# State-space input laid out through DRAM, phase tables as one tile, read-out matrices earlier on POOL

## The chip, the cores and the metric

The kernel runs on one core of a Trainium2 chip. The core has a matrix engine (TensorE, PE in the profile), a vector engine (VectorE, DVE), a scalar engine (ScalarE, ACT), GpSimd (POOL) and SyncE (SP), which issues the transfers here. Each engine works through its own queue of instructions in order; between engines semaphores hold an instruction back until its inputs are there and the memory it writes is free. The metric is the device time of one execution in microseconds (us); lower is better.

## What is computed

The reference is one layer of a diffusion backbone for 128 context and 512 latent tokens (640 columns in all) of width 1024. Of the combined projection `z = h @ w_in` come the inputs of three mixers: attention, a bidirectional linear recurrent unit (`lru`), and a bidirectional state-space mixer (S5). Only the last one is changed:

```python
lam_bar = jnp.exp(lam * step)
b_bar = ((lam_bar - 1.0) / lam)[..., None] * b_mat[None]
bu = jnp.einsum('blgp,dgnp->dblgn', u32.astype(jnp.complex64), b_bar)
for d, reverse in enumerate((False, True)):
    a = jnp.broadcast_to(lam_bar[d], bu[d].shape)
    h, h_last = linear_scan(a, bu[d], h0[:, d], reverse)
    y = y + jnp.einsum('blgn,gpn->blgp', h, c_mat[d]).real
```

After it come the merge gates, the output projection and a convolutional feed-forward network, which take the rest of the time.

## The kernel before

Activations lie with the width on the 128 partitions and the 640 tokens along the free axis. Each large product is made of three products of split operands: `hh`/`hl` are the high and low part of an activation, `sh`/`sl` those of a weight block. For each block of weights SP loads `wr` (512 KB), ACT writes `sh`, DVE writes `sl = wr - sh`, and PE multiplies; so PE asks ACT, DVE and SP for something every few microseconds in the whole kernel.

The state-space mixer works on four tokens at a time (160 columns of four). Its parts, in order of the program:
- `u`, the mixer's input: two products of 128 rows; ACT copies each out of PSUM into `usb`, and 16 copies on DVE (L660) spread it into `ut`, where token 0 to 3 of a group of four stand on four blocks of 32 partitions. `usb` has the tag `xh` with one buffer, so the `xh` of the first `lru` tile lies in the same memory and is written after the last copy.
- `s5_prepare`: for each direction `d`, POOL clears `vt` (L334), DVE fills it with 8 copies, 12 products and 12 sums, PE forms `gp` from it and transposes it into `vm`; at the end DVE and ACT assemble `km`.
- `s5_tables` (DVE): the phase tables `tab0` and `tab1`, real and imaginary powers for 160 columns, by doubling: from n columns the next n, in blocks of 16 at most, each block with six operations through two scratch tiles `tq`; five small operations square the power.
- `s5_cl` (POOL): the read-out matrices `cl`, in eight rounds of two products into scratch tiles and four sums into `cl`, 48 operations. Its scratch tiles have the tags of the tables' scratch.
- `s5_half`, twice, each for two directions: PE multiplies `vm` by `ut`, ACT moves the result to `v`, DVE rotates it by the tables, scans it twice and rotates it back to `sr` and `si` (this is called a chain here: from `v<-v,lh0r` to `si`), and PE sums `ut,km`, `sr,cl` and `si,cl`.

The order of POOL's queue is that of the program (`manual_schedule`); the other queues are ordered by a scheduler that knows of costs. The program itself interleaves the preparation (`p`) with the two `lru` tiles by the string `ORDER`, and between any two steps `fill()` emits independent work (gate products, modulation, the attention's values):

```python
    for g in ORDER:
        next(gens[g], None)
        fill()
```

The pool `pst`, with `vt` and the other tiles of the preparation, is closed before `ptab`, the pool of the tables, is opened; both take memory from the same side.

Of the kernel before, what the change touches and what calls it, by code (L numbers as in the profile page):

```python
# [11 lines left out]
F32 = mybir.dt.float32  # L12
# [8 lines left out]
P = 128  # L21
# [17 lines left out]
KPOW = 1  # L39
NB = 2  # L40
# [29 lines left out]
def tile_hybrid_flow_step(ctx, tc, a, o):  # L70
# [241 lines left out]
    def s5_prepare(pst):  # L312
# [11 lines left out]
        t4 = [pst.tile(sh, F32, name=f"q{i}") for i in range(4)]  # L324
# [175 lines left out]
    vct = pv.tile([P, 512], F32, name="vct")  # L500
    tsp = [pd.tile([P, NT], F32, name=f"tsp{i}") for i in range(24)]
# [237 lines left out]
    tab = [ptab.tile([P, 16, 160], F32, name=f"tab{q}") for q in range(2)]  # L739

    def s5_tables(e):

        er, ei = tab
        V.memset(er[:, :, 0:1], 1.0)
        V.memset(ei[:, :, 0:1], 0.0)
        p_r, p_i = unit
        n = 1
        while n < 160:
            for z in range(0, min(n, 160 - n), 16):
                m = min(16, n - z)  # L750
                tmp = [ptab.tile([P, 16, 16], F32, tag=f"tq{q}", name="tq") for q in range(2)]
                br = p_r.unsqueeze(2).to_broadcast([P, 16, m])
                bi = p_i.unsqueeze(2).to_broadcast([P, 16, m])
                t0, t1 = (t[:, :, 0:m] for t in tmp)
                tt(t0, er[:, :, z:z + m], br, MUL, e)
                tt(t1, ei[:, :, z:z + m], bi, MUL, e)
                tt(er[:, :, n + z:n + z + m], t0, t1, SUB, e)
                tt(t0, er[:, :, z:z + m], bi, MUL, e)
                tt(t1, ei[:, :, z:z + m], br, MUL, e)
                tt(ei[:, :, n + z:n + z + m], t0, t1, ADD, e)  # L760
            n *= 2
            if n < 160:
                q = [pl.tile([P, 16], F32, tag=f"q{z}", name="q", bufs=2) for z in range(3)]
# [5 lines left out]
                p_r, p_i = q[0], q[1]  # L769

    def s5_cl(e):

        for w in range(1, 5):
            lr, nli = bc(lamp[w][0]), bc(nlam[w])
            for ri, (x, y, op) in enumerate(((lr, nli, ADD), (nli, lr, SUB))):
                t0 = ptab.tile([P, 2, 8, 16], F32, tag="tq0", name="tq")
                t1 = ptab.tile([P, 2, 8, 16], F32, tag="tq1", name="tq")
                tt(t0, cc[0], x, MUL, e)
                tt(t1, cc[1], y, MUL, e)
                for g in range(2):  # L780
                    rows = slice(64 * g, 64 * g + 64)
                    for d in range(2):
                        slot = w - 1 if d == 0 else 4 - w
                        tt(cl[rows, d, ri, :, slot, g, :], t0[rows, d], t1[rows, d], op, e)

# [854 lines left out]
```

## Time and profile before

| what | value |
|---|---|
| median of three runs | 1060.23 us (1059.8 to 1065.33) |
| the profiled execution | 1060.12 us |
| its span in the trace | 1058.3 us |
| mean granted clock of TensorE | 0.971 of full speed |
| PE busy | 999.2 us, 94% of the span |
| DVE busy | 813.3 us, 77% |
| ACT busy | 460.5 us, 44% |
| POOL busy | 148.6 us, 14% |
| PE busy from 60 to 240 us | 163.0 of 180 us, granted clock 0.93 |
| PE busy from 240 to 490 us | 249.3 of 250 us, granted clock 1.00 |

The span counts from the first to the last instruction in the trace; the time of the execution holds 1.8 us more. The state-space mixer's preparation and first chains lie between 60 and 240 us. In rows of the trace a line reads: start, duration, engine, line of the program, operation, tile written, tiles read, count, and in brackets how long the engine sat idle before and for whom. Two levels of TensorE's clock appear in it, 1.00 (2.4 GHz) and 0.50 (1.2 GHz).

### The profile page before, as it was taken

Reading aid. Unit: us, or ns where it says so; the run is one execution under the profiler, and the core shown is the slowest. Engines: PE = TensorE matmul, PEld = TensorE weight load, DVE = VectorE, ACT = ScalarE, POOL = GpSimd, SP = SyncE. Lnnn points to the kernel's source line nnn. Section 1 sums busy time; section 2 is a strip of 40 time slices with the busy share of each in tenths; the row PEclk is TensorE's granted clock in tenths of the full one; section 3 lists DMA queues with packets and bytes.
Section 4 is the critical chain, followed back from the end, with each engine's and each line's share of the span. In section 5 each row is a group of like instructions: output and inputs, shape, how many; then the busy total and the mean of one; then the engine's idle time right before and its main releaser. Section 6 shows DMA issues by size and latency. Waiting matters only on the chain. (4 is left out here: it accounts for less than half of the span.)

```text
span 1058.3 us, 17728 instructions
## 1 busy us (share of the span) xinstructions
PE 999.2 (94%) x6620; PEld 929.8 (88%) x6620; DVE 813.3 (77%) x1954; ACT 460.5 (44%) x876; POOL 148.6 (14%) x147
## 2 busy tenths in 40 slices
PE   6998999779999999999979987999999999999995
PEld 4798986659999999998979886988999899988994
DVE  6897788956856766566676888976998589966977
ACT  5245362214345655455222544542555145522544
POOL 6010001950002011020000231100110001100104
PEclk9999999889999999999989988999999999999998
DMA  9532277544334324345964033240234122331212
GB/s 366 212 91 80 71 240 238 184 143 130 112 100 160 103 83 138 96 98 133 261 215 144 21 59 102 81 135 25 80 87 133 60 62 84 98 97 59 81 60 100
DMA packets 49798, 127.62 MB, mean 121 GB/s; under 512 B 5552, under 2 KB 16688, under 8 KB 49712
## 3 DMA queue, kind: packets, MB, share of 16 engines
q1 hardware_dynamic: 49008, 124.37, 37.8%
q0 software_dynamic: 704, 2.11, 0.8%
q8 instruction: 52, 0.85, 0.3%
q14 instruction: 34, 0.28, 0.1%
HBM read 113.06 MB, written 12.09 MB: 118 GB/s over the span
## 5 line engine op out<-in xcount | busy, mean ns | idle before, releaser
L77 ACT ACTIVATE sh<-wr 128x512 fp32r<-128x512 f32 (+1 forms) x300 | 181.5, 618 | 247.3 <-PE dn L92 87.6
L80 DVE TENSOR_TENSOR sl<-wr,sh 128x512 fp32r<-128x512 f32 (+1 forms) x300 | 209.1, 704 | 79.5 <-ACT sh L77 78.3
L92 PE MATMUL bk<-hh,sl 128*128 128x320 f32 x608 | 190.6, 315 | 6.3 <-DVE sl L80 6.2
L92 PE MATMUL bk<-hl,sh 128*128 128x320 f32 x608 | 189.9, 313 | 0.0
L92 PE MATMUL bk<-hh,sh 128*128 128x320 f32 x608 | 187.4, 316 | 1.2 <-ACT sh L77 1.0
L92 PEld LDWEIGHTS bk<-hh,sl 128*128 128x128 f32 x608 | 116.0, 191 | 11.3 <-DVE sl L80 8.2
L92 PEld LDWEIGHTS bk<-hh,sh 128*128 128x128 f32 x608 | 114.7, 191 | 11.9 <-issue 4.6
L92 PEld LDWEIGHTS bk<-hl,sh 128*128 128x128 f32 x608 | 116.2, 191 | 1.6 <-DVE Z L86 0.8
L92 PE MATMUL bM<-xth,sl 128*128 128x320 f32 x352 | 109.6, 312 | 6.5 <-DVE sl L80 6.5
L92 PE MATMUL bM<-xth,sh 128*128 128x320 f32 x352 | 109.6, 311 | 1.5 <-ACT M L77 1.0
L92 PE MATMUL bM<-xtl,sh 128*128 128x320 f32 x352 | 109.1, 310 | 0.0
L92 PE MATMUL dn<-sl,ah 128*128 128x512 f32 (+1 forms) x224 | 87.4, 390 | 0.0
L92 PE MATMUL dn<-sh,al 128*128 128x512 f32 (+1 forms) x224 | 87.3, 390 | 0.0
L92 PE MATMUL dn<-sh,ah 128*128 128x512 f32 (+1 forms) x224 | 87.2, 389 | 0.0
L92 PE MATMUL bM<-xbh,sh 128*128 128x320 f32 x264 | 82.6, 314 | 0.0
L92 PE MATMUL bM<-xbh,sl 128*128 128x320 f32 x264 | 82.5, 313 | 0.0
L92 PE MATMUL bM<-xbl,sh 128*128 128x320 f32 x264 | 82.2, 312 | 0.1
L80 POOL TENSOR_TENSOR wr<-wr,s 128x512 f32<-128x512 f32 x20 | 31.5, 1575 | 333.4 <-DVE sl L80 288.7
L92 PEld LDWEIGHTS bM<-xth,sl 128*128 128x128 f32 x352 | 66.7, 190 | 7.4 <-DVE sl L80 7.2
L92 PEld LDWEIGHTS bM<-xth,sh 128*128 128x128 f32 x352 | 66.7, 189 | 2.0 <-ACT M L77 1.2
L92 PEld LDWEIGHTS bM<-xtl,sh 128*128 128x128 f32 x352 | 66.6, 189 | 0.0
L77 ACT ACTIVATE tgate<-bk 128x320 f32<-128x320 f32 x48 | 20.6, 430 | 73.4 <-PE bk L92 48.2
(364 smaller groups left out, 2245.6 us busy)
## 6 DMA issues: line engine op xcount, KB each, us to landing
wr<-in_w_up SPq DMA_DIRECT2D x44, 512.0 KB
wr<-in_w_in SPq DMA_DIRECT2D x38, 512.0 KB
wr<-in_w_ada SPq DMA_DIRECT2D x32, 512.0 KB
wr<-in_w_down SPq DMA_DIRECT2D x22, 512.0 KB
adw<-in_w_ada SPq DMA_DIRECT2D x16, 512.0 KB
tsp<-tgate SPq DMA_DIRECT2D x24, 320.0 KB
tg<-tsp SPq DMA_DIRECT2D x24, 320.0 KB
wr<-in_w_out SPq DMA_DIRECT2D x8, 512.0 KB
```

What stands on the lines that cost most here:

```text
L77: S.activation(out, in_, f, **k)
L80: e.tensor_tensor(out, x, y, op)
L92: T.matmul(out, l, r, start=start, stop=stop)
```

## The change

Four things change.
- `u` goes through DRAM. ACT writes `usb` with the four tokens of a group apart, SP stores it to a scratch tensor `udr` (320 KB), and four loads of 80 KB bring it to the partitions of `ut`. The 32 copies on DVE go away.
- The two tables become one tile `tab`, with real and imaginary part side by side. A block takes three operations of twice the size instead of six, and squaring the power three instead of five.
- `s5_cl` is emitted at the seventh step of the preparation, which is behind POOL's second clearing of `vt`, instead of behind the tables, and its scratch tiles `cq` now lie in `pst`.
- `t4`, the four scratch tiles `q` of the preparation, share memory with scratch tiles of an earlier product.

```diff
@@ s5_prepare
-        t4 = [pst.tile(sh, F32, name=f"q{i}") for i in range(4)]
+        t4 = [pst.tile(sh, F32, tag=f"cm{i + 1}b", name="q") for i in range(4)]
@@ the state-space input
+    udr = pd.tile([2, P, 4, 160], F32, name="udr")
...
-        u = pl.tile([P, NT], F32, tag="xh", name="usb", bufs=1)
+        u = pl.tile([P, 4, 160], F32, tag="xh", name="usb", bufs=1)
         for h in range(2):
-            act(u[:, h * HT:(h + 1) * HT], b[h][:, :HT])
-        uv = u.rearrange("p (c t) -> p t c", t=4)
-        for j in range(4):
-            for t0 in range(4):
-                V.tensor_copy(ut[32 * t0:32 * t0 + 32, 4 * i + j], uv[32 * j:32 * j + 32, t0])
+            act(u[:, :, 80 * h:80 * h + 80], b[h][:, :HT].rearrange("p (c t) -> p t c", t=4))
+        Q.dma_start(out=udr[i], in_=u)
+        for t0 in range(4):
+            Q.dma_start(out=ut[32 * t0:32 * t0 + 32, 4 * i:4 * i + 4],
+                        in_=udr[i].rearrange("(j f) t c -> t f j c", f=32)[t0])
@@ s5_cl: moved up, its two scratch tiles now in pst
-                t0 = ptab.tile([P, 2, 8, 16], F32, tag="tq0", name="tq")
-                t1 = ptab.tile([P, 2, 8, 16], F32, tag="tq1", name="tq")
+                t0 = pst.tile([P, 2, 8, 16], F32, tag="cq0", name="cq")
+                t1 = pst.tile([P, 2, 8, 16], F32, tag="cq1", name="cq")
@@ the order of emission
+    steps = 0
     for g in ORDER:
         next(gens[g], None)
+        if g == "p":
+            steps += 1
+            if steps == CL_AT:
+                s5_cl(G)
         fill()
@@ s5_tables
-    tab = [ptab.tile([P, 16, 160], F32, name=f"tab{q}") for q in range(2)]
+    tab = ptab.tile([P, 2, 16, 160], F32, name="tab")
...
-                t0, t1 = (t[:, :, 0:m] for t in tmp)
-                tt(t0, er[:, :, z:z + m], br, MUL, e)
-                tt(t1, ei[:, :, z:z + m], bi, MUL, e)
-                tt(er[:, :, n + z:n + z + m], t0, t1, SUB, e)
-                tt(t0, er[:, :, z:z + m], bi, MUL, e)
-                tt(t1, ei[:, :, z:z + m], br, MUL, e)
-                tt(ei[:, :, n + z:n + z + m], t0, t1, ADD, e)
+                x = tab[:, :, :, z:z + m]
+                tt(t0, x, pw_[:, 0:1].unsqueeze(3).to_broadcast(sh), MUL)
+                tt(t1, x[:, ::-1], pw_[:, 1:3].unsqueeze(3).to_broadcast(sh), MUL)
+                tt(tab[:, :, :, n + z:n + z + m], t0, t1, ADD)
             n *= 2
             if n < 160:
-                tt(q[2], p_i, p_i, MUL, e)
-                tt(q[0], p_r, p_r, MUL, e)
-                tt(q[0], q[0], q[2], SUB, e)
-                tt(q[1], p_r, p_i, MUL, e)
-                tt(q[1], q[1], q[1], ADD, e)
+                tt(sq, pw_[:, 0::2], pw_[:, 0::2], MUL)
+                tt(q[:, 0], sq[:, 0], sq[:, 1], SUB)
+                stt(q[:, 1:3], pw_[:, 1:3], 2.0, pw_[:, 0:1].to_broadcast([P, 2, 16]), MUL, MUL)
...
-    s5_tables(TE)
-    s5_cl(G)
+    s5_tables()
```

Three places of the queues show what this moves.

The first is SP's queue where `u` is ready, some 70 to 100 us into the span. Before:

```order
L110 DMA wr<-in_w_v 128x1024 x2
L110 DMA wr<-in_w_in 128x1024
L110 DMA wr<-in_w_ada 128x1024
L524 DMA vdr<-vs 128x256 x3
L110 DMA wr<-in_w_ada 128x1024
L524 DMA vdr<-vs 128x256
```

After:

```order
L111 DMA wr<-in_w_v 128x1024 x2
L659 DMA udr<-usb 128x640
L111 DMA wr<-in_w_in 128x1024
L661 DMA ut<-udr 32x4x160 x4
L111 DMA wr<-in_w_ada 128x1024
L659 DMA udr<-usb 128x640
L661 DMA ut<-udr 32x4x160 x4
L526 DMA vdr<-vs 128x256 x3
L111 DMA wr<-in_w_ada 128x1024
```

Each half's store is followed by its four loads, the first with a weight load between. A load of `wr<-in_w_ada` now stands behind the loads of the first half, the store of the second half behind that load, and the stores of `vs` behind the loads of the second half.

The second place is POOL and DVE from the second clearing of `vt` on; the names in brackets are the engines' semaphores that an instruction waits for (DMAHW is a transfer's). POOL before:

```order
L323 MEMSET cb 128x1024 [waits DVE_49,Activation_49]
L334 MEMSET vt 128x2048 [waits DMAHW6_49,DMAHW4_49,PE_49]
L334 MEMSET vt 128x2048 [waits DVE_49,PE_49,Pool_49]
L80 TENSOR_TENSOR tq<-pk,lp_94 128x256 [waits DMAHW4_49,DMAHW1_49,DVE_49]
L80 TENSOR_TENSOR tq<-pk,nl_102 128x256
L80 TENSOR_TENSOR cl<-tq 64x8x16 [waits Pool_49]
L80 TENSOR_TENSOR cl<-tq 64x8x16 x3
```

POOL after:

```order
L324 MEMSET cb 128x1024 [waits DVE_49,Activation_49]
L335 MEMSET vt 128x2048
L335 MEMSET vt 128x2048 [waits DVE_49,PE_49,Pool_49]
L81 TENSOR_TENSOR cq<-pk,lp_94 128x256 [waits DMAHW1_49]
L81 TENSOR_TENSOR cq<-pk,nl_102 128x256
L81 TENSOR_TENSOR cl<-cq 64x8x16 [waits Pool_49]
L81 TENSOR_TENSOR cl<-cq 64x8x16 x3
```

The first product behind the second `MEMSET vt` waited for DVE (the tables' last use of the scratch) and now waits only for a load of long ago. DVE before, at the end of the preparation:

```order
L384 COPY km<-dg 32x8x32
L80 TENSOR_TENSOR sl<-wr,sh 128x512 [waits DMAHW1_49,Activation_49]
L80 TENSOR_TENSOR sl<-wr,sh 128x512 [waits Activation_49]
L744 MEMSET tab_2158 128x16 [waits PE_49]
L745 MEMSET tab_2159 128x16 [waits DVE_49]
L80 TENSOR_TENSOR tq<-tab_2158,unr 128x16 [waits DVE_49]
L80 TENSOR_TENSOR tq<-tab_2159,uni 128x16 [waits DVE_49]
```

DVE after:

```order
L385 COPY km<-dg 32x8x32
L81 TENSOR_TENSOR sl<-wr,sh 128x512 [waits DMAHW3_49,Activation_49]
L81 TENSOR_TENSOR sl<-wr,sh 128x512 [waits Activation_49]
L765 MEMSET tab 128x16 [waits DVE_49,PE_49,Pool_49]
L766 MEMSET tab 128x16
L768 COPY pw__2204<-unr 128x16
L769 COPY pw__2204<-uni 128x16
L87 TENSOR_SCALAR pw__2204<-uni 128x16
```

The first operation of the tables waited for PE alone and now waits for POOL as well; the count that it waits for is that of the last of the 48 operations of `s5_cl`, since `tab` lies in the memory of the preparation's `vt` and `cq`. The rest of the tables, the gates of the second `lru` tile and the following `sl` stand behind it.

The third place is DVE at the first chain, some 185 us into the span. Before:

```order
L80 TENSOR_TENSOR v<-v,lh0r 128x4
L80 TENSOR_TENSOR tb<-v,tab_2158 128x640
L80 TENSOR_TENSOR tb<-v,tab_2159 128x640
L80 TENSOR_TENSOR v<-v,lh0i 128x4
L80 TENSOR_TENSOR sl<-wr,sh 128x512
L80 TENSOR_TENSOR tb<-v,tab_2159 128x640
L80 TENSOR_TENSOR tb<-v,tab_2158 128x640
L80 TENSOR_TENSOR tb<-tb 128x640 x2
L836 SCALAR_TENSOR_TENSOR v<-rho,tb 128x640 x2
```

After:

```order
L81 TENSOR_TENSOR sl<-wr,sh 128x512 x2
L81 TENSOR_TENSOR v<-v,lh0r 128x4
L81 TENSOR_TENSOR tb<-v,tab 128x640 x2
L81 TENSOR_TENSOR v<-v,lh0i 128x4
L81 TENSOR_TENSOR tb<-v,tab 128x640 x2
L81 TENSOR_TENSOR tb<-tb 128x640 x2
L839 SCALAR_TENSOR_TENSOR v<-rho,tb 128x640 x2
L81 TENSOR_TENSOR tb<-v,tab 128x640 x4
L81 TENSOR_TENSOR sr<-tb 128x4x159
```

The second `sl`, which stood inside the chain, now stands with the first ahead of it; the next pair of `sl` follows the chain in both. On PE the order is nearly the same: single products with `si,cl` and `ut,km` move by a few places, and `gp`, `ut,vm` and the weight products stay where they were.

## Rows read from the trace of the kernel before

**Rows 1.** Waits of PE, 80 to 250 us: total us, times, longest us.
```profile
PE bk L92 <- DVE sl L80: 5.9, 2, 5.4
PE bk L92 <- POOL cl L80: 5.3, 2, 4.4
PE bk L92 <- ACT xh L77: 3.8, 1, 3.8
```

**Rows 2.** Windows: from:to, length, busy of PE, PEld, DVE, ACT, POOL; PEclk; DMA.
```profile
89.57:92.98 3.41, 2.89 (x11) 2.82 (x11) 1.30 (x8) 1.48 (x4) 0.00 (x0) 0.50 0.23 77
202.21:209.04 6.83, 3.60 (x13) 3.60 (x14) 6.83 (x15) 0.93 (x3) 6.61 (x8) 0.50 0.44 164
222.69:229.52 6.83, 3.96 (x15) 3.96 (x16) 2.02 (x10) 0.00 (x0) 3.10 (x6) 0.50 0.41 152
```

**Rows 3.** Timeline of ACT, last of `usb`, first `xh`: start, duration, [idle before <- for whom].
```profile
79.65 0.43 ACT L77 ACTIVATE usb<-bk 128x320 f32<-128x320 f32 x1
...
88.43 0.74 ACT L77 ACTIVATE xh<-xc 128x642 fp32r<-128x642 f32 x1 [8.08 <-DVE ut L660]
```

**Rows 4.** Timeline of DVE: the first chain, beside POOL; and a later one, alone.
```profile
186.64 0.17 DVE L80 TENSOR_TENSOR v<-v,lh0r 128x4 f32<-128x4 f32 x1 [0.22 <-ACT v L77]
...
197.43 4.16 DVE L80 TENSOR_TENSOR tb<-v,tab 128x640 f32<-128x640 f32 x4
...
257.08 0.17 DVE L80 TENSOR_TENSOR v<-v,lh0r 128x4 f32<-128x4 f32 x1 [1.01 <-ACT v L77]
...
264.69 3.00 DVE L80 TENSOR_TENSOR tb<-v,tab 128x640 f32<-128x640 f32 x4
...
268.34 0.81 DVE L80 TENSOR_TENSOR si<-tb 128x636 f32<-128x636 f32 x1
```

**Rows 5.** Timeline of POOL: second `vt`, then the read-out matrices (`tq`, `cl`).
```profile
115.98 1.81 POOL L334 MEMSET vt<- 128x2048 f32 x1 [59.19 <-PE vtp L364]
180.97 0.62 POOL L80 TENSOR_TENSOR tq<-pk,lp 128x256 f32<-128x256 f32 x1 [63.18 <-DVE si L857]
...
182.25 1.81 POOL L80 TENSOR_TENSOR cl<-tq 64x128 f32<-64x128 f32 x4
184.13 0.62 POOL L80 TENSOR_TENSOR tq<-pk,nl 128x256 f32<-128x256 f32 x1
...
198.00 3.91 POOL L80 TENSOR_TENSOR cl<-tq 64x128 f32<-64x128 f32 x4
...
223.36 2.56 POOL L80 TENSOR_TENSOR cl<-tq 64x128 f32<-64x128 f32 x4
```

**Rows 6.** Timelines of SP and ACT: a weight load of 512 KB and its reader.
```profile
180.88 0.33 SPq L110 DMA_DIRECT2D wr<-in_w_in  x1
...
184.38 0.63 ACT L77 ACTIVATE sh<-wr 128x512 fp32r<-128x512 f32 x1 [3.98 <-DMA wr<-in_w_in]
```

**Rows 7.** Timeline of PE: `gp` of the second `vt`; two products with a new `sl`.
```profile
125.47 3.65 PE L92 MATMUL gp<-cb,vt 128*128 128x32 f32 x32
...
150.05 0.41 PE L92 MATMUL bk<-hh,sl 128*128 128x320 f32 x1
...
205.44 0.63 PE L92 MATMUL bk<-hh,sl 128*128 128x320 f32 x1 [5.36 <-DVE sl L80]
```

**Rows 8.** Timeline of DVE: last `vt` sums, tables' start, first gate operation, `sl`, tables' end.
```profile
122.24 0.98 DVE L80 TENSOR_TENSOR vt<-q,q 64x128 f32<-64x128 f32 x4
...
136.81 0.07 DVE L744 MEMSET tab<- 128x16 f32 x1 [0.67 <-PE vtp L364]
...
144.95 1.56 DVE L83 SCALAR_TENSOR_TENSOR tg<-tg,xc 128x642 f32<-128x642 f32 x2
...
149.31 0.68 DVE L80 TENSOR_TENSOR sl<-wr,sh 128x512 fp32r<-128x512 f32 x1
...
179.67 0.76 DVE L80 TENSOR_TENSOR tq<-tab,q 128x256 f32<-128x256 f32 x2
...
185.04 0.84 DVE L80 TENSOR_TENSOR sl<-wr,sh 128x512 fp32r<-128x512 f32 x1 [4.13 <-ACT sh L77]
```

More of the change, by code (lines that the diff above doesn't have):

```diff
@@ L39 @@
 KPOW = 1
+CL_AT = 7
 NB = 2
@@ L725, in lru_tile, with s5_cl @@
         ylru.append(y)
+    def s5_cl(e):
+        for w in range(1, 5):
+            lr, nli = bc(lamp[w][0]), bc(nlam[w])
+            for ri, (x, y, op) in enumerate(((lr, nli, ADD), (nli, lr, SUB))):
+                t0 = pst.tile([P, 2, 8, 16], F32, tag="cq0", name="cq")
+                t1 = pst.tile([P, 2, 8, 16], F32, tag="cq1", name="cq")
+                tt(t0, cc[0], x, MUL, e)
+                tt(t1, cc[1], y, MUL, e)
+                for g in range(2):
+                    rows = slice(64 * g, 64 * g + 64)
+                    for d in range(2):
+                        slot = w - 1 if d == 0 else 4 - w
+                        tt(cl[rows, d, ri, :, slot, g, :], t0[rows, d], t1[rows, d], op, e)
     gens = {"p": prep, "0": lru_tile(0), "1": lru_tile(1)}
+    steps = 0
     for g in ORDER:
         next(gens[g], None)
+        if g == "p":
+            steps += 1
+            if steps == CL_AT:
+                s5_cl(G)
         fill()
@@ L738, in tile_hybrid_flow_step, with s5_tables @@
     es_b, ptab = pool("ptab", side="left")
-    tab = [ptab.tile([P, 16, 160], F32, name=f"tab{q}") for q in range(2)]
[L741 to L746, printed above, removed]
+    tab = ptab.tile([P, 2, 16, 160], F32, name="tab")
+    def s5_tables():
+        V.memset(tab[:, 0, :, 0:1], 1.0)
+        V.memset(tab[:, 1, :, 0:1], 0.0)
+        pw_ = ptab.tile([P, 3, 16], F32, tag="pw", name="pw_", bufs=2)
+        V.tensor_copy(pw_[:, 0], unit[0])
+        V.tensor_copy(pw_[:, 2], unit[1])
+        ts(pw_[:, 1], unit[1], -1.0, None, MUL, ALU.bypass)
         n = 1
@@ L750, in s5_tables @@
                 m = min(16, n - z)
-                tmp = [ptab.tile([P, 16, 16], F32, tag=f"tq{q}", name="tq") for q in range(2)]
-                br = p_r.unsqueeze(2).to_broadcast([P, 16, m])
-                bi = p_i.unsqueeze(2).to_broadcast([P, 16, m])
-                t0, t1 = (t[:, :, 0:m] for t in tmp)
-                tt(t0, er[:, :, z:z + m], br, MUL, e)
-                tt(t1, ei[:, :, z:z + m], bi, MUL, e)
-                tt(er[:, :, n + z:n + z + m], t0, t1, SUB, e)
-                tt(t0, er[:, :, z:z + m], bi, MUL, e)
@@ L759, in s5_tables @@
-                tt(t1, ei[:, :, z:z + m], br, MUL, e)
-                tt(ei[:, :, n + z:n + z + m], t0, t1, ADD, e)
+                sh = [P, 2, 16, m]
+                t0, t1 = (ptab.tile([P, 2, 16, 16], F32, tag=f"tq{q}", name="tq")[:, :, :, 0:m] for q in range(2))
+                x = tab[:, :, :, z:z + m]
+                tt(t0, x, pw_[:, 0:1].unsqueeze(3).to_broadcast(sh), MUL)
+                tt(t1, x[:, ::-1], pw_[:, 1:3].unsqueeze(3).to_broadcast(sh), MUL)
+                tt(tab[:, :, :, n + z:n + z + m], t0, t1, ADD)
@@ L761, in s5_tables @@
             n *= 2
             if n < 160:
-                q = [pl.tile([P, 16], F32, tag=f"q{z}", name="q", bufs=2) for z in range(3)]
-                tt(q[2], p_i, p_i, MUL, e)
-                tt(q[0], p_r, p_r, MUL, e)
-                tt(q[0], q[0], q[2], SUB, e)
-                tt(q[1], p_r, p_i, MUL, e)
-                tt(q[1], q[1], q[1], ADD, e)
[L769 to L775, printed above, removed]
-                t0 = ptab.tile([P, 2, 8, 16], F32, tag="tq0", name="tq")
-                t1 = ptab.tile([P, 2, 8, 16], F32, tag="tq1", name="tq")
[L778 to L784, printed above, removed]
@@ L786, in tile_hybrid_flow_step @@
-    s5_tables(TE)
-    s5_cl(G)
+                q = ptab.tile([P, 3, 16], F32, tag="pw", name="pw_", bufs=2)
+                sq = ptab.tile([P, 2, 16], F32, tag="pq", name="pq")
+                tt(sq, pw_[:, 0::2], pw_[:, 0::2], MUL)
+                tt(q[:, 0], sq[:, 0], sq[:, 1], SUB)
+                stt(q[:, 1:3], pw_[:, 1:3], 2.0, pw_[:, 0:1].to_broadcast([P, 2, 16]), MUL, MUL)
+                pw_ = q
+    s5_tables()
     for i in range(2):
@@ L806, in s5_half @@
             sel = slice(8 * d + j0, 8 * d + j0 + 4)
-            er, ei = tab[0][:, sel], tab[1][:, sel]
+            er, ei = tab[:, 0, sel], tab[:, 1, sel]
             tmp = [p5.tile(sh, F32, tag=f"tb{q}", name="tb") for q in range(4)]
```

## The prediction

> **What bounds the kernel now.** TensorE (PE) is busy 94% of the span and from 240 to 490 us it works 249.3 of 250 us (both in the table ahead): no later wait is there that could swallow what is won or lost ahead of it, so a wait that PE loses before 240 is taken from the end, and a new one is added to it. I read the waits of PE next [rows 1]: between 80 and 250 us three places carry nearly all of the waiting, and the change touches each of them. ACT's `xh` holds PE 3.8 us; VectorE's (DVE's) `sl`, a low half of split weights, holds it 5.4 us once; POOL's `cl` holds it 5.3 us in two waits. Then I read the granted clock behind each wait [rows 2]: it shows 0.50, the 1.2 GHz level, for 3.41 us behind the first, and for 6.83 us around each of the others, of which 3.60 and 3.96 us are PE at work. Work at that level takes twice as long, so half of PE's busy time there is lost too.
>
> Of every PE wait I then looked at what the waited-for engine did. ACT's `xh` sat idle 8.08 us for `ut` [rows 3]: the copies `ut<-usb` on DVE read the tile that `xh` is about to overwrite. The `sl` of the second place stands behind a whole state-space chain on DVE, which runs beside POOL's `cl` and is stretched by it: the four products take 4.16 us there and 3.00 us later, alone [rows 4]. POOL's `cl` starts at 180.97, having waited 63.18 us for the phase tables, whose scratch it shares, and four of its operations take 3.91 us beside DVE and 1.81 alone [rows 5].
>
> **What goes.** All terms are made against the profiled execution, 1060.12 us (span 1058.3), which is within 0.01% of the median 1060.23.
> A, `u` through DRAM. The 32 copies leave DVE, so `xh` no longer waits for them, but for the second store `udr<-usb`. Its source is complete when ACT has read the second half of `u` out of PSUM, now at 79.65 + 0.43 [rows 3] and not later without the copies, so I put its issue at 80.1. A load of 512 KB takes 184.38 - 180.88 = 3.50 us from issue to its reader [rows 6]; the store is 320 KB to DRAM, and the trace does not show one with a reader, so I bound it by that row at 3.5 us, and by twice it at 7. At 3.5 `xh` may start by 83.6 and is done by 84.4; PE asks for it at 88.43 + 0.74 - 3.8 = 85.4 [rows 1, 3]: the wait goes. At 7 most of it stays. I take 3.5, the row of nearest size. Worth 3.8 us, 0.5 for `xl` behind it, and half of the 2.89 us of PE work at the low clock: 5.8. The eight loads `ut<-udr` are needed about 100 us later and hold up only the short SP queue.
> B, the `sl` at 205.44. With POOL's work gone from here, the chain takes 268.34 + 0.81 - 257.08 = 12.1 us [rows 4]. It starts at 186.64 as before (it needs PE's `ut,vm`), ends at 198.7, some small copies and one `sl` of 0.69 follow, 200.1; PE, which waits 5.36 us until 205.44 [rows 7], asks at 200.1. I leave 0.2. Worth 5.4 + 3.60/2 - 0.2 = 7.0.
> C, `cl`. It is there early, and PE then waits for the second chain instead. That follows the first by about 13.7 us (12.1, copies, two `sl`) and ends near 212.5; PE, without B's loss, gets there near 212. I leave 1.0. Worth 5.3 + 3.96/2 - 1.0 = 6.3.
> Sum of the gains: 19.1.
> The wide tables. A block of 16 columns costs two rounds of a pair of 0.76 and one of 0.42, 2.5 us as they follow each other [rows 8]; after, a pair and one operation of 128x512, and one operation of that size (an `sl`) costs 0.68 [rows 8], so a pair about 1.3 and the block 2.0. Nine such blocks, some 4.5 us of DVE. This is worth nothing by itself: DVE sits 4.13 us behind the tables for ACT's `sh`, which waits for a load [rows 6, 8]. Bounds: 0 and, if that cover were gone, 4.5 of gain. I take 0.
>
> **What is added.** POOL's 48 operations now start together with DVE's second filling of `vt`, and the order shows a new wait: `MEMSET tab`, the first operation of the tables, waits for the last of the 48, since `tab` lies where `vt` and `cq` lay. Behind it in DVE's queue stand the tables, all gate arithmetic of the second `lru` tile, and the `sl` that PE needs. So POOL's end, call it P, decides. In times of the trace of before (what A shifts, it shifts for all of them alike):
> - Start: `MEMSET vt`, 115.98 + 1.81 = 117.8 [rows 5].
> - Alone, a round of six operations takes 184.13 - 180.97 = 3.16 us, eight rounds 25.3 [rows 5]. P is at least 143.1.
> - Beside DVE: four products took 4.16 us instead of 3.00, and four `cl` 3.91 instead of 1.81 [rows 4, 5], so one DVE operation of 0.74 and one POOL operation of 0.45 follow each other every 1.02 us; of POOL's 0.45 some 0.28 excludes DVE. A DVE operation of length d then makes a POOL operation last d + 0.28. For the 24 fillings of `vt` (0.98 us for four [rows 8]) that is 0.05 each, 1.3; for the eight operations of 0.6 to 0.74 or less between there and the tables (`tg`, three `sl`, `y`, `dg`) and four short copies, 3.3. Together 4.6, P = 147.7. Bounds: nothing, 143.1; or in proportion to DVE's work: now the 48 take 223.36 + 2.56 - 180.97 = 45.0 us [rows 5], 19.7 more than alone, beside two chains and some `sl`, about 28 us of DVE work; that is 0.7 us for each of the 10.3 us of such work here, 150.3. I take the middle one, since most operations are short.
> - `MEMSET tab` ran at 136.81, and PE's first matmul with the next `sl` (started 149.31, 0.68 long) began at 150.05, 0.06 us after that `sl` was done [rows 7, 8]: DVE was already the last to arrive there and had worked without a pause since 136.81. So a lag of DVE at the tables is a wait of PE at 150, one for one: 147.7 - 136.8 = 10.9.
> - Ahead of the first gate operation (144.95 [rows 8]) the tables take 8.1 us now and by the order about 8.7 after: 0.6. By the third pair of `sl` behind it DVE has by the order one wide operation more than now ahead of it: 0.7.
> - Behind a wait of this size the clock is low for about 3.4 us of work [rows 2]: 1.7.
> Sum: 13.9. The fillings of `vt` are stretched too, by up to 0.28 x 24 = 6.7 us, and PE asks for them at 125.47 [rows 7], 2.3 us after they end now (122.24 + 0.98 [rows 8]); this wait of up to 4.4 us is inside the 10.9, not beside it.
>
> The same row tells how hard the two engines exclude each other. The Trainium skill, "SBUF — State Buffer", section "SBUF: two separate sides", says that a DVE operation with two SBUF inputs and a GpSimd operation that reads SBUF hold their shared ports as an exclusive lock for the whole instruction. By it a pair would take 0.74 + 0.45 = 1.19 us, and the trace shows 1.02: it agrees that they take turns, not that nothing overlaps. The rule's own outcome is a rival below.
>
> **The sum.** 1060.1 - 19.1 + 13.9 = 1054.9. Of a change of this kind a measurement can tell about 0.5%, 5.3 us; the forecast lies on that bound.
>
> **Rivals.**
> POOL runs free. P = 143.1, cost 9.3, **1050.3**. For it: small DVE operations beside POOL are often not delayed, and DVE stalls at `tab`, out of POOL's way. Against it: the 24 fillings come one right behind the other.
> The stall is not paid in full. DVE catches up between the tables and 150, and only the `vt` wait (up to 4.4 us and 1.7 of clock) is left: **1047**. Against it: DVE shows no pause there.
> Whole operations exclude each other. POOL loses all of DVE's 10.3 us: P = 153.4, cost 19.6, **1060.6**. For it: the turns in the trace. Against it: the 1.02. This is the outcome of the skill's rule named above.
> The DRAM way is too long: A stays, 1054.9 + 5.8 = **1060.7**. The change then does not do what it says, at this place. Against it: more than 1 us of slack by the loads seen.
> Slower: POOL's 48 operations take as long as now, 45 us. P = 162.8, cost 29, **1070**. It decides from P = 153 on (gain used up), and the time is over the bound from P = 158. For it: they took that long beside DVE. Against it: that was beside 28 us of DVE work, and here there are 10, then DVE stands still.
>
> **How the numbers follow.** Forecast 0.50 (1052 to 1058, half of it on either side of the 0.5% bound at 1054.9); POOL free 0.15; stall not paid 0.08; whole operations 0.12; A stays 0.07; slower 0.08. Faster: 0.25 + 0.15 + 0.08 = 0.48. Same: 0.25 + 0.12 + 0.07 = 0.44. Slower: 0.08. The range from 1047 to 1062 leaves out the slower case and the lower part of the stall's: 0.84 lies in it.
>
> **What would show it.** Right: in the profile after, no PE wait for `xh` near 85; `MEMSET tab` at about 142 (6 us earlier by the clock of the new run than the 147.7), with DVE idle before it for POOL's `cl`; a PE wait of some 5 to 10 us for `sl` near 145 to 155, that was not there; no wait for `cl`, chains of 12 us, waits of 1 us or less where 5.4 and 5.3 stood; POOL's 48 operations in about 30 us. Wrong: DVE reaching `tab` after POOL is done (no wait: then about 1047); a store to DRAM that ends after 84; or chains still near 17 us without POOL beside them, which would take away B and C.

## The result

The changed kernel takes 1051.5 us (median of four runs, 1049.5 to 1054.4) where the kernel before takes 1061.7 on the same chip; the ratio is 0.9889, with a 95% interval of 0.9864 to 0.9914. Measured again beside another version, with more runs, it was 0.9906 (0.9890 to 0.9923). So it is faster by about 1%, 10 to 12 us. The forecast was 1054.9 us in a range from 1047 to 1062: the time lies in the range, and the gain is twice the forecast 5.2 us. The profiled execution after took 1052.65 us (span 1050.9), that of before 1060.12; the latter was one of the fastest of its kernel, and later groups of runs had medians of 1064 to 1065 for it, so what follows compares ratios and, in traces, places.

One line of the page after, as in the table of before (columns: busy us, share of the span, instructions):

```profile
PE 997.6 (95%) x6620; PEld 927.6 (88%) x6620; DVE 796.3 (76%) x1872; ACT 461.6 (44%) x876; POOL 132.0 (13%) x147
```

PE works nearly as long as before (997.6 us, where it was 999.2); the span is shorter mostly because it waits less. Its waits from 74 to 245 us, which answer to [rows 1]:

```profile
PE gp L93 <- DVE vt L81: 4.1, 2, 4.0
PE bk L93 <- ACT sh L78: 1.7, 1, 1.7
PE bk L93 <- DVE sl L81: 1.5, 2, 0.9
```

The three waits of before are gone: no `xh`, no `cl`, and of `sl` two small ones are left. One wait is new, 4.0 us for `vt`, and one for ACT's `sh` has grown to 1.7 us. The stretches of low clock in the same place of the program, which answer to [rows 2] (columns as there):

```profile
122.56:132.80 10.24, 10.24 (x45) 8.51 (x46) 6.73 (x12) 2.62 (x7) 9.68 (x18) 0.50 0.26 72
177.17:180.59 3.42, 3.42 (x13) 2.56 (x10) 1.89 (x5) 0.00 (x0) 0.00 (x0) 0.50 0.63 238
```

The three stretches of before are gone as well, and so is a fourth that stood at 113.5. Behind the new wait there is one of 10.24 us, all of it PE at work, so half of it, 5.1 us, is lost. (The one at 177 was at 174.9 before.)

**Part A** took the wait away, as the prediction says. SP's queue and ACT, which answer to [rows 3]:

```profile
79.00 0.38 SPq L659 DMA_DIRECT2D udr<-usb  x1
83.59 1.74 SPq L661 DMA_DIRECT2D ut<-udr  x4
```

```profile
77.13 0.42 ACT L78 ACTIVATE usb<-bk 128x320 f32<-128x320 f32 x1
...
83.68 0.74 ACT L78 ACTIVATE xh<-xc 128x642 fp32r<-128x642 f32 x1 [3.68 <-DMA udr<-usb]
```

The second half of `u` is complete at 77.55 (77.13 + 0.42), 2.5 us ahead of the forecast 80.1. Its store goes out only at 79.00, right behind a weight load in SP's queue (78.55), and from there to the start of `xh` it takes 4.7 us where the forecast has 3.5. Its loads go out at 83.59, and `xh` starts at 83.68 (it was 88.43). That the forecast says 83.6 is luck: the three errors cancel.

**POOL and DVE between 110 and 140.** POOL's 48 operations, which answer to [rows 5], and DVE beside them, to [rows 8]:

```profile
110.55 0.66 POOL L81 TENSOR_TENSOR cq<-pk,lp 128x256 f32<-128x256 f32 x1
...
111.87 1.87 POOL L81 TENSOR_TENSOR cl<-cq 64x128 f32<-64x128 f32 x4
...
122.32 2.78 POOL L81 TENSOR_TENSOR cl<-cq 64x128 f32<-64x128 f32 x4
...
136.92 2.13 POOL L81 TENSOR_TENSOR cl<-cq 64x128 f32<-64x128 f32 x4
```

```profile
110.64 2.19 DVE L350 COPY vt<-bar 64x128 f32<-64x128 f32 x4
112.84 2.37 DVE L81 TENSOR_TENSOR vt<-q 64x128 f32<-64x128 f32 x4
...
120.40 2.00 DVE L81 TENSOR_TENSOR vt<-q 64x128 f32<-64x128 f32 x4
...
129.46 0.85 DVE L391 COPY km<-gp 32x256 f32<-32x256 f32 x2
...
131.52 1.75 DVE L385 COPY km<-dg 32x256 f32<-32x256 f32 x3
...
139.13 0.15 DVE L768 COPY pw__2204<-unr 128x16 f32<-128x16 f32 x1 [1.74 <-PE vtp L365]
139.14 0.07 DVE L765 MEMSET tab<- 128x16 f32 x1
...
151.56 0.68 DVE L81 TENSOR_TENSOR sl<-wr,sh 128x512 fp32r<-128x512 f32 x1
```

POOL starts at 110.55 and ends at 139.05, 28.5 us; the forecast was 29.9, and alone it would be 25.3. DVE's 24 fillings take from 110.64 to 122.40, 11.8 us instead of 5.4: four take 1.6 to 2.4 us where they took 0.73 to 0.99. Beside them POOL loses only about 1 of its 3.2 us (122.32 - 111.87 is three rounds in 10.45 us, alone 9.5). So there the cost of the exclusion falls nearly all on DVE. Not every operation of DVE pays: the same two groups of copies at the end of the preparation, in the trace of before and without POOL beside them, are

```profile
129.61 0.85 DVE L390 COPY km<-gp 32x256 f32<-32x256 f32 x2
...
131.37 0.88 DVE L384 COPY km<-dg 32x256 f32<-32x256 f32 x3
```

The copies of `gp`, which lies in PSUM, take 0.85 us with and without POOL; those of `dg`, which lies in SBUF, take 1.75 instead of 0.88. `MEMSET tab` starts at 139.14. The trace names PE for the wait ahead of it; in the rows of PE the transposes that it names end at 138.36, and POOL's last `cl` ends at 139.05, so POOL came last, by 0.7 us.

```profile
121.91 0.38 PE L93 MATMUL gp<-cb,vt 128*128 128x32 f32 x2 [3.98 <-DVE vt L81]
...
136.39 1.97 PE L365 MATMUL vtp<-ident,vt 128*128 128x128 f32 x16
...
152.29 0.42 PE L93 MATMUL bk<-hh,sl 128*128 128x320 f32 x1 [0.63 <-DVE sl L81]
```

PE waits 3.98 us at `gp`, where it had 2.3 us in hand, and then only 0.63 at the `sl` of 151.56. That is where the forecast put the great wait.

**The chains**, which answer to [rows 4]:

```profile
189.03 0.17 DVE L81 TENSOR_TENSOR v<-v,lh0r 128x4 f32<-128x4 f32 x1
...
196.63 3.01 DVE L81 TENSOR_TENSOR tb<-v,tab 128x640 f32<-128x640 f32 x4
...
200.29 0.82 DVE L81 TENSOR_TENSOR si<-tb 128x636 f32<-128x636 f32 x1
...
202.63 0.16 DVE L81 TENSOR_TENSOR v<-v,lh0r 128x4 f32<-128x4 f32 x1
```

From 189.03 to 201.11 the first chain takes 12.1 us, the second starts at 202.63, and PE waits for neither.

### The profile page after: what moved, and what is told of

It reads as the page before. It is cut to its first block, busy times and chain, and to the rows that moved or that the text cites. A ratio compares the mean times of both kernels' runs of the same rounds, so it can differ in the third digit from the quotient of the medians.

```text
span 1050.9 us, 17655 instructions
## 1 busy us (share of the span) xinstructions
PE 997.6 (95%) x6620; PEld 927.6 (88%) x6620; DVE 796.3 (76%) x1872; ACT 461.6 (44%) x876; POOL 132.0 (13%) x147
## 4 chain that ended last, share of the span: by engine, by line
PE 41%; DVE 3%; DMA 2%; issue 2%; ACT 1%; POOL 1%; POOLq 0%; ACTq 0%; DVEq 0%
PE bM L93 23%; PE dn L93 13%; PE bk L93 5%; DMA wr<-in_w_up 1%; DVE x L81 1%; DMA tg<-tsp 1%; DVE xtl L81 0%; PE bk L1200 0%; DVE sl L81 0%; POOL rs L81 0%; DVE dt L81 0%; ACT sq L78 0%; POOL wr L81 0%; ACT sh L78 0%; DVE yo L1416 0%
## 5 line engine op out<-in xcount | busy, mean ns | idle before, releaser
L93 PE MATMUL bk<-sl,mh 128*128 128x256 f32 x160 | 46.8, 294 | 5.5 <-DVE sl L81 5.5
```

Of the source, the lines that this page charges most:

```text
L93: T.matmul(out, l, r, start=start, stop=stop)
```

## Where the time went, place by place

The lead of the changed kernel, read at the same product of PE in both traces:

| at the product (time before) | lead | what lies between |
|---|---|---|
| first products with `xh`, behind the low clock (93) | 6.1 us | `xh`, `xl`, low clock |
| behind the transposes of the first `vt` (117) | 7.7 | the low clock at 113.5 is gone |
| second `gp` (125.5) | 3.6 | lost: the wait for `vt` |
| end of the low clock (131) | -1.5 | lost: 5.1 of low clock |
| `ut,vm` (178) | -3.0 | lost: small waits for `sl`, ACT's `sh` and `m`, 3.2 us in sum where 1.6 stood |
| behind the first chain (208) | 4.3 | `sl`, and low clock |
| behind `cl` (229) | 12.8 | `cl`, and low clock |
| 480 | 12.3 | |
| 660 | 7.3 | (see the experiments) |

So up to 230 us the change wins 7.7, loses 10.7 and wins 15.8.

## Experiments

The theory: the early place of POOL's work wins the waits for `sl` and `cl`, and costs some 10 us because DVE is kept from filling the second `vt`. Its rivals: the order or the tables made the chains short, not POOL's absence; or PE is simply early at `vt`; or the exclusion can't be escaped, wherever POOL's work stands. Ratios are to the kernel before, each on the same chip as its group; "lead" is the lead at 480 us against the trace of the kernel before.

| kernel | ratio (95%) | lead at 480 |
|---|---|---|
| changed kernel | 0.9889 (0.9864 to 0.9914) | 12.3 |
| e1: POOL's work late again | 0.9903 (0.9878 to 0.9927) | 7.2 |
| e2: at step 2 | 0.9949 (0.9933 to 0.9965) | 4.7 |
| e3: `u` by copies | 0.9918 (0.9894 to 0.9942) | 7.6 |
| e4: narrow tables | 0.9873 (0.9838 to 0.9907) | 13.4 |
| e5: split, shared scratch | 0.9874 (0.9854 to 0.9893) | 14.0 |
| e6: POOL's work left out | 0.9797 (0.9777 to 0.9817) | 21.1 |
| e7: all behind the first filling, shared scratch | 0.9924 (0.9904 to 0.9943) | 10.3 |
| e8: kernel before with wide tables alone | 0.9953 (0.9936 to 0.9970) | 1.9 |
| e9: split, own scratch | 0.9813 (0.9764 to 0.9861) | 20.4 |
| e10: all behind the first filling, own scratch | 0.9830 (0.9791 to 0.9869) | 15.0 |
| e11: changed kernel again | 0.9906 (0.9890 to 0.9923) | 12.7 |
| e12: e9 again | 0.9811 (0.9794 to 0.9828) | 16.3 |

(Each lead is that of one profiled execution. Some of them start their first work late, which is in the lead: by 1.3 us in e1 and e12, by 2.7 to 3.3 us in e2, e8 and e10, read at 36 us; the others by less than 1 us. The change's fourth part, shared scratch for `t4`, was not run by itself.)

### e1: POOL's work behind the tables again

```diff
-                t0 = pst.tile([P, 2, 8, 16], F32, tag="cq0", name="cq")
+                t0 = ptab.tile([P, 2, 8, 16], F32, tag="tq0", name="tq")
...
             if steps == CL_AT:
-                s5_cl(G)
+                pass
...
     s5_tables()
+    s5_cl(G)
```

> The changed kernel with one part undone: the 48 POOL operations stand behind the tables again, with their scratch in the tables' memory. Theory: the early place buys the second and third gain (the `sl` behind the first chain, and `cl`: some 14 us at 230 us into the span) and costs some 10 us between 118 and 178 (DVE kept from filling `vt`, a wait of PE of 4 us and 10 us of low clock behind it). Undone, both go: no PE wait for `vt`, no low clock at 122 to 133, PE waits of about 5 us for `sl` and 5 us for `cl` back, chains near 17 us; the start of the first chain is 6 to 7 us ahead of the kernel before; the time 1052 to 1057. Rival: the chains got short because the tables or the order changed, not because POOL left; then the waits stay away, and with the `vt` wait gone too the time is 1040 to 1045.

Measured 1054.2 us, ratio 0.9903. PE's waits, and the two ends of DVE's first chain:

```profile
PE bk L93 <- DVE sl L81: 5.8, 3, 4.7
PE bk L93 <- POOL cl L81: 1.6, 1, 1.6
```

```profile
181.73 0.41 DVE L81 TENSOR_TENSOR v<-v,lh0r 128x4 f32<-128x4 f32 x1
...
197.19 1.07 DVE L81 TENSOR_TENSOR si<-tb 128x636 f32<-128x636 f32 x1
```

The first chain takes 16.5 us (181.73 to 198.26), where it took 17.1 before (186.64 to 203.74) and 12.1 in the changed kernel, with the tables and the order of the changed kernel: it was POOL's absence that made the chains short. The long `sl` (4.7) is back, and so is the low clock behind it, and PE does not wait for `vt`: as the theory says. But of `cl` only 1.6 us came back, not 5.3. In this kernel POOL starts at 173.25; the lead there is 3 to 4 us, so that is some 4 us earlier in the program than before, because the wide tables, for whose end it waits, end earlier. So the early place, in the end, is worth 0 to 1.5 us of the whole gain (0.9889 and 0.9906 against 0.9903; the intervals overlap), and some 4 us by the leads with e1's late start set aside: most of what it wins at 200 to 230 us it loses at 118 to 133.

### e8: the wide tables alone

```diff
-    s5_tables(TE)
+    s5_tables()
     s5_cl(G)
```

(with the new body of `s5_tables`, in the kernel before)

> The kernel before with one part of the change alone: the tables as one tile with wide operations; `u` by copies, the POOL operations behind the tables. Theory now: POOL's start waits for the tables' end, so each us that the tables save is a us that `cl` is less late; they save about 4, and PE's two waits for `cl` (5.3 us) shrink to 2 or less: 1053 to 1058. Rival (what the prediction said): the saving lies in DVE's wait for a load behind the tables and is worth nothing: 1059 to 1062.

Measured 1059.9 us, ratio 0.9953: 5 us for an edit that the prediction priced at nothing. (The time by itself lies in the range of the rival; but the kernel before took 1065.0 us beside it, not the 1060 to 1062 from which both ranges were made.) POOL's first operation, and PE's waits:

```profile
179.10 0.62 POOL L80 TENSOR_TENSOR tq<-pk,lp 128x256 f32<-128x256 f32 x1 [58.58 <-DVE modt L80]
```

```profile
PE bk L92 <- DVE sl L80: 5.6, 3, 4.6
...
PE bk L92 <- DVE sr L858: 1.7, 1, 1.7
```

The trace of this run started its work some 3 us late, so 179.10 is about 176 in times of the trace of before, where it was 180.97 [rows 5]: POOL starts 5 us earlier. PE no longer waits for `cl`; what is left there is 1.7 us for `sr` of the second chain.

### e4: narrow tables in the changed kernel

```diff
-    s5_tables()
+    s5_tables(TE)
```

(with two tables `tab0`, `tab1` and the old body)

> The changed kernel with one part undone: two tables, six operations of 128x256 for each block. Theory: the tables have cover (a load is waited for behind them), and DVE reaches the gate operations after the same 8.1 us: no difference, 1050 to 1054, and PE's waits as in the changed kernel to within 1 us. Rival: DVE is the bound from 139 us on, and the 4.5 us that the wide operations save reach PE by the `sl` between the tables: 1055 to 1058, with PE waits for `sl` between 150 and 180 longer by 2 to 4 us.

Measured 1050.3 us, ratio 0.9873, and a lead of 13.4 us at 480: no difference. With POOL's work out of the way nothing waits for the tables' end, and the same edit is worth nothing. The two edits are two ways to take the same wait.

### e3: `u` by copies in the changed kernel

```diff
-        Q.dma_start(out=udr[i], in_=u)
-        for t0 in range(4):
-            Q.dma_start(out=ut[32 * t0:32 * t0 + 32, 4 * i:4 * i + 4], ...
+        for j in range(4):
+            for t0 in range(4):
+                V.tensor_copy(ut[32 * t0:32 * t0 + 32, 4 * i + j], uv[32 * j:32 * j + 32, t0])
```

> The changed kernel with one part undone: the 32 copies on DVE lay out `u` again, no DRAM. Theory: the wait of PE for `xh` (3.8 us, with 0.5 for `xl` and the low clock behind it, 6 us together) comes back whole, and all that follows is shifted alike: 1056 to 1060. Rival: the later waits for `vt` and `sl` swallow it, since POOL and DVE set the time there: 1050 to 1053.

Measured 1056.3 us, ratio 0.9918: 1 to 3 us slower than the changed kernel; the lead at 480 is smaller by 4.7.

```profile
PE gp L93 <- DVE vt L81: 4.0, 1, 4.0
PE bk L93 <- ACT xh L78: 3.8, 1, 3.8
```

```profile
127.54:141.20 13.66, 13.02 (x55) 11.26 (x56) 9.85 (x18) 3.00 (x8) 12.88 (x24) 0.50 0.35 113
```

`xh` costs 3.8 us again, as the theory has it, and the wait for `vt` is 4.0 as with the DRAM way: PE is not early at `vt` because of part A. The low clock behind `vt` is 13.66 us here, longer than in the changed kernel. The ratio's difference is less than the 6 us expected, and its interval (0.9894 to 0.9942) does not settle how much less.

### e6: POOL's work left out

```diff
             if steps == CL_AT:
-                s5_cl(G)
+                pass
```

> The changed kernel without the 48 POOL operations: the read-out matrices are left at zero, so the output lacks the state's part; PE multiplies by them as ever. It shows what they cost where they stand now. Theory: the filling of the second `vt` takes 5.4 us instead of 12, PE's wait of 4.0 us for it and 10 us of low clock behind it go, the tables start as soon as PE's transposes are done; at 240 us some 22 us ahead of the kernel before, the time 1036 to 1043. Rival: with the gain of the first part PE is simply early for `vt`, whoever works beside DVE; the wait stays at 2 us or more with low clock behind it, and the time is 1046 to 1052.

Measured 1043.7 us, ratio 0.9797, 10 us under the changed kernel. PE's largest waits from 74 to 245 us (two, 0.9 at most):

```profile
PE bk L93 <- DVE sl L81: 1.1, 2, 0.9
```

PE does not wait for `vt`, and of low clock there is one stretch of 3.4 us from 74 to 245 us: so the wait is POOL's doing, and the cost of the 48 operations where the change puts them is 0.9889 or 0.9906 less 0.9797, that is 10 to 11.5 us.

### e2: POOL's work at step 2

```diff
-CL_AT = 7
+CL_AT = 2
```

> The changed kernel with the 48 POOL operations emitted at step 2 of the preparation instead of step 7, which is between the two clearings of `vt`, from about 58 us on. Theory: what the early place costs is the exclusion of DVE while it fills the second `vt`; with POOL elsewhere, the filling takes 5.4 us, PE does not wait for it, the clock stays up, and at 240 us the kernel is some 20 us ahead of the kernel before instead of 12.8; some of it is given back between 490 and 640 us; the time 1040 to 1046. Rival: the exclusion only moves, and the `sl` of the weight products at 60 to 77 us come late instead, PE waiting there for about 5 to 10 us; the time 1049 to 1056.

Measured 1059.0 us, ratio 0.9949: the rival's mechanism came, at a time over its range. The waits of PE from 50 us on, one of DVE's small operations, and the store of `u` with its reader:

```profile
PE bk L93 <- DVE sl L81: 6.7, 4, 3.5
PE bk L93 <- ACT xh L78: 3.9, 1, 3.9
```

```profile
64.59 0.58 DVE L87 TENSOR_SCALAR sps<-sps 128x4 f32<-128x4 f32 x1
```

```profile
95.88 0.38 SPq L659 DMA_DIRECT2D udr<-usb  x1
```

```profile
100.66 0.74 ACT L78 ACTIVATE xh<-xc 128x642 fp32r<-128x642 f32 x1 [10.61 <-DMA udr<-usb]
```

POOL now runs from 59 to about 92 us, beside a stretch in which DVE has many small operations. A scalar operation on 4 columns, 0.16 us elsewhere, takes 0.58; the `sl` among them come late (6.7 us of PE waiting). `xh` comes late (3.9) by way of SP's queue: it waits for the second store of `u`, which goes out at 95.88, right behind a weight load that went out at 95.43 (in the changed kernel 79.00 and 78.55). At 93 us the kernel is 12.4 us behind that of before, 2.7 of them by its late start; it wins the chains later.

### e5 and e7: POOL held back until DVE is idle, first form

```diff
-        t4 = [pst.tile(sh, F32, tag=f"cm{i + 1}b", name="q") for i in range(4)]
...
         for d in range(2):
+            t4 = [pst.tile(sh, F32, tag=f"cm{i + 1}b", name="q") for i in range(4)]
...
-                t0 = pst.tile([P, 2, 8, 16], F32, tag="cq0", name="cq")
+                t0 = pst.tile([P, 2, 8, 16], F32, tag="cm3b", name="cq")
...
-            if steps == CL_AT:
-                s5_cl(G)
+            if steps == 5:
+                s5_cl(G, (1, 2))
+            if steps == 11:
+                s5_cl(G, (3, 4))
```

(e7: all four powers at step 5.)

> The changed kernel with the 48 POOL operations in two halves, each held back until DVE has filled a `vt`: rounds for the first two powers behind the first filling (about 78 us, when DVE stands still for `xh`), the others behind the second (about 117 us). Their scratch shares memory with the scratch that the filling's sums read, which makes POOL wait for DVE. Theory (the exclusion of DVE during a filling is the cost): the second filling takes 5.4 us, no PE wait for `vt`, no low clock at 122 to 133, no wait for `cl` later, and no PE wait for `sl` at 80 to 90; at 240 us some 18 to 22 us ahead of the kernel before; the time 1038 to 1046. Rival: wherever POOL's 28 us stand before 180 us, DVE loses as much as now and PE waits at another place: 1048 to 1056.

> The changed kernel with all 48 POOL operations behind the first filling of `vt` (about 78 us, held by the same sharing of scratch) and ahead of the second clearing. Theory: they have 30 us until the second clearing is due at 109, and DVE has some 12 us of idle time there; `xl` and the gates of the first `lru` tile are stretched by 0.3 us an operation, POOL is done near 107 to 110, so the second `vt` is late by 2 us at most and PE waits 1 us or less for it: 1040 to 1047. Rival: the stretch of `xl`, of the gates and of the `sl` between 84 and 100 reaches PE, waits of 3 us or more in sum with low clock behind them: 1048 to 1055.

Measured 1051.5 us (0.9874) and 1056.4 us (0.9924): about the numbers of the rivals, but not by their mechanism. DVE in e5, and in e7:

```profile
91.45 0.49 DVE L81 TENSOR_TENSOR q<-bar,lp 128x128 f32<-128x128 f32 x2 [11.18 <-POOL cl L81]
91.86 0.82 DVE L81 TENSOR_TENSOR xl<-xc,xh 128x642 fp32r<-128x642 f32 x1
```

```profile
103.48 0.49 DVE L81 TENSOR_TENSOR q<-bar,lp 128x128 f32<-128x128 f32 x2 [17.51 <-POOL cl L81]
...
105.36 0.69 DVE L81 TENSOR_TENSOR sl<-wr,sh 128x512 fp32r<-128x512 f32 x1
```

The edit itself put a wait in: the first products of the second filling write the scratch that POOL now reads, stand early in DVE's queue, and wait 11.18 us in e5 and 17.51 in e7 for POOL. In e5 `xl` stands behind them and PE waits 6.6 us; in e7 an `sl`, and PE waits 9.6. So these two say nothing on exclusion, but they show the queue: what waits at the head of an engine's queue holds up all that stands behind it.

### e9 and e10: the same with scratch of its own

```diff
-            t4 = [pst.tile(sh, F32, tag=f"cm{i + 1}b", name="q") for i in range(4)]
+            t4 = [pst.tile(sh, F32, tag=f"q{i}" if d else f"cm{i + 1}b", name="q") for i in range(4)]
...
-                s5_cl(G, (3, 4))
+                s5_cl(G, (3, 4), ("q2", "q3"))
```

(against e5 and e7; the last pair of lines is e9 alone, whose second half has the scratch of the second filling)

> The same split as in e5_cl_split (24 POOL operations behind the first filling of `vt`, 24 behind the second), but the products of the second filling have scratch of their own, so DVE no longer waits for POOL's first half with `xl` queued behind. Theory (the exclusion during a filling is what the early place costs, and e5 lost its gain to that wait of 6.6 us): no PE wait above 1 us between 80 and 130, no low clock from 88 to 96; at 240 us 18 to 22 us ahead of the kernel before; the ratio to the kernel before 0.980 to 0.985. Rival: POOL's first half, running while DVE makes `xl` and the gates of the first `lru` tile, costs PE as much as in e5 and e7 by exclusion alone: the ratio 0.987 to 0.993.

> All 48 POOL operations behind the first filling of `vt`, as in e7_cl_slot1, with the second filling's products on scratch of their own. Theory: e7 lost 9.6 us to an `sl` that stood on DVE behind products that waited for POOL; without that wait POOL runs from 77 to about 106, beside `xl` and the gates, each of whose operations is stretched by about 0.3 us, PE waits 2 us or less in sum between 80 and 125; the second `vt` is in time and the tables do not wait for POOL: the ratio to the kernel before 0.979 to 0.986. Rival: exclusion of the gates and of the `sl` between 84 and 106 reaches PE with 4 us or more and low clock behind: the ratio 0.987 to 0.993.

Measured 1044.1 us, ratio 0.9813, for the split, and 1047.3 us, 0.9830, for the undivided one. The largest wait of PE in e9, and DVE's last sums of the second `vt` with the start of the tables:

```profile
PE bk L93 <- DVE sl L81: 1.1, 2, 0.9
```

```profile
116.91 0.99 DVE L81 TENSOR_TENSOR vt<-q 64x128 f32<-64x128 f32 x4
...
133.24 0.07 DVE L767 MEMSET tab<- 128x16 f32 x1
```

No wait above 0.9 us is left, the last four sums take 0.99 us again, and the low clock at this place is one stretch of 3.4 us. The lead of 20.4 us is within 0.7 of that of e6, where POOL's 48 operations are left out: most of what the exclusion costs can be escaped, by giving POOL's work times in which DVE mostly stands still or reads PSUM. Both times came as their theories have it. In e10 POOL took 37.6 us, not some 29 (80.09 to 117.69), and PE still waited for nothing longer than 0.9 us. That scratch of its own for the second filling would help without the new places was not run; in the changed kernel no filling waits for scratch.

### e11 and e12: both again, side by side

> The changed kernel once more, beside the split version on one chip, for a direct comparison: the ratio to the kernel before 0.986 to 0.992, as measured before.

> The split version of e9_cl_split_free once more. Theory: it keeps what the change wins and loses nothing to the exclusion, so it stands 0.006 to 0.009 (some 6 to 10 us) under the changed kernel on the same chip: the ratio to the kernel before 0.978 to 0.984. Rival: its 1044 us was a lucky set of runs, and it lies within 0.003 of the changed kernel.

Measured 1054.0 us (0.9906) and 1044.7 us (0.9811, 0.9794 to 0.9828). The split version is faster than the changed kernel by 0.0095 of the time before, some 10 us, a little more than expected, and than the kernel before by 20. In the trace of e12 PE again does not wait for `vt`; its lead is smaller than e9's by more than the late start (17.6 and 20.7 us without it), so a lead of one trace is good to some 3 us.

### What the stretch from 490 to 660 us shows

The changed kernel's lead falls from 12.3 to 7.3 us there. One long wait of DVE for a transfer in it, and PE's longest wait (for an `sl` whose weights DVE waited for, 8.5 and 9.9 us), in the trace of before and then in that of after:

```profile
512.86 0.89 DVE L83 SCALAR_TENSOR_TENSOR acc<-tg,bk 128x320 f32<-128x320 f32 x2 [7.32 <-DMA tg<-tsp]
```

```profile
641.74 0.63 PE L92 MATMUL bM<-xth,sl 128*128 128x320 f32 x1 [6.54 <-DVE sl L80]
```

```profile
501.67 0.89 DVE L84 SCALAR_TENSOR_TENSOR acc<-tg,bk 128x320 f32<-128x320 f32 x2 [8.41 <-DMA tg<-tsp]
```

```profile
634.43 0.63 PE L93 MATMUL bM<-xth,sl 128*128 128x320 f32 x1 [7.90 <-DVE sl L81]
```

Each wait is 1.1 to 1.4 us longer after, and a stretch of low clock between them lasts 13.65 us (525.33 to 538.98) where it lasted 10.24 (536.71 to 546.95). But it isn't gain given back: all kernels above lose 1.8 to 5 us in this stretch against the one trace of before, e8, with a lead of 1.9 us, loses 4.2, and e9, with 20.4, loses 2.8. The trace of before is that of an execution at the low end of its kernel's runs, 1060.1 us where their medians were 1061.7 to 1065.0; that this stretch is where it was good fits, but without a second trace of that kernel it is not shown. The gain of the medians, 10 to 12 us, is near the lead at 480. What makes these loads land earlier or later from run to run wasn't tried.

## Why the prediction was right, and where it was not

- **A, 5.8 forecast.** Right in mechanism; the time of `xh` was met by luck, since an earlier `usb`, a wait in SP's queue and a slower store (4.7 us for 3.5) cancelled. Measured 6.1 behind the wait, 7.7 at 117 us, since a low clock behind the first `gp` (113.5 to 116.9 in the trace of before) went too; e3 puts the part's worth at 4.7 us of lead, and at 1 to 3 us by the ratios.
- **B and C, 13.3 forecast.** Right in mechanism: chains of 12.1 us, no wait for `cl`. e1, with POOL late again, has both back in part. Measured 15.8; the 1.2 us that I left for new waits were not there, and some small waits beside the two went with them.
- **The new wait, 13.9 forecast.** The step that named POOL's end was right: the 48 took 28.5 us where it has 29.9, and the tables waited for the last of them. (By its own rule a filling of 0.245 us would add 0.075 to a POOL operation of 0.45, not 0.05; that is half a microsecond, and nothing hung on it.) The step behind it, a lag of DVE as one wait of PE of 10.9 us at 150, was wrong. PE waited 0.63 us there, because it was itself late by then: 4.0 us at `vt`, which the prediction counted as "inside the 10.9", and 5.1 by the clock behind it. The mis-sized term is the clock: I took 3.4 us of low clock behind a wait from [rows 2], 1.7 us lost, and it was 10.24 us. DVE was late at the tables by 9.5 us (139.14 for 136.81, and 7.2 for the earlier start of `vt`), PE by 9.2; since they were late side by side, PE's cost was 10.7 us, not their sum. That this is near the forecast 13.9 is in part luck: nothing in the prediction foresaw two lags of one size.
- **The wide tables, nothing forecast.** Right for this kernel (e4), for a reason that the prediction named only by half: they have cover behind them on DVE, but POOL waited for their end, and [rows 5] showed that wait of 63.18 us. Alone they are worth 5 us (e8).
- **No swallowing later.** The prediction looked at 240 to 490 us, where PE hardly waits, and concluded that no later wait could swallow the gain. Up to 490 it holds: the lead is 12.4 us at 250 and 12.3 at 490. What lies behind 490 it did not look at; there the traces lose 1.8 to 5 us, whatever their lead.
- **The rivals.** "POOL runs free" was nearest in time (1050.3) and false in mechanism: DVE was excluded nearly as far as the bound of 6.7 us that the prediction gave (6.4 measured). "The stall is not paid in full" (1047) was nearest in what PE lost: the wait for `vt` with its clock, and nearly nothing at 150. With 5.1 us of clock for its 1.7 it gives 1050.5. But DVE did not catch up, as that rival has it; PE was late itself. "Whole operations exclude each other" did not come: by it POOL would have lost all the time that DVE works, about 10 us, and the trace shows 3.2. One behind the other, the fillings (5.4 us) and the 20 POOL operations beside them (20 of 48, 10.5 of 25.3 us) would take 15.9 us, and they took 11.8. The rule behind this rival, in the Trainium skill, "SBUF — State Buffer", section "SBUF: two separate sides", is that the one that starts first gets the shared ports for its whole instruction and the other is fully blocked. The trace agrees that each holds up the other (DVE by 6.4 us, POOL by 3.2), not that nothing overlaps.

The errors add up as 1.9 (A), 2.5 (B and C) and 3.2 us (the wait), all to the same side: a lead of 12.8 us where 5.2 was forecast. The time lies in the range, but each of the three terms was too cautious.

## What to carry to other kernels

Moving work to an idle engine has its price where the two slow each other, as DVE and POOL do here: give it the stretches in which the other engine stands still, and hold it there by scratch that it must wait for, but look what else in the other's queue then waits for that scratch. When two edits aim at one wait (a producer that ends sooner, a consumer that no longer waits for it), price them together: alone each may be worth it all, and both no more than one. And count a wait of TensorE with the clock behind it, read at that very place if a trace shows one.

## What was not expected of the hardware

- The low clock behind waits of like length was not of like length. Behind 4.71 us of waiting it lasted 3.42 us in e1, where products of 320 columns follow (the row below); behind 3.98 us, where the 32 small products of `gp` follow, 10.24 us in the changed kernel and 13.66 in e3. What decides it was not tried.

```profile
200.01:203.43 3.42, 3.42 (x13) 3.42 (x14) 3.39 (x6) 0.00 (x0) 3.28 (x5) 0.50 0.31 110
```

- Exclusion between DVE and POOL fell mostly on the engine with the shorter operations. For small ones of DVE it is one-sided: a filling of 64 partitions by 128 columns went from 0.24 to 0.50 to 0.59 us, an operation on 4 columns from 0.16 to 0.42 to 0.58 (e2), while POOL's 48 operations went from 25.3 to 28.5 us. Beside products of 640 columns POOL lost more: four `cl` took 3.91 us instead of 1.81, DVE's four products 4.16 instead of 3.00 [rows 4, 5].
- A store of 320 KB to DRAM, with the wait of its reader, took 4.7 us (79.00 to 83.68); the first of the two took 4.1 (70.53 to 74.63).
